# Partial sums issued between two sweeps, and another split of the FFN's blocks into groups

## The chip, the cores and the metric

The kernel runs on one core of one Trainium2 chip. The metric is the device time of one execution in microseconds (us), and the time of a kernel is the median of its runs. The engines are TensorE (PE, with its weight loads as PEld), VectorE (DVE), ScalarE (ACT), GpSimd (POOL) and SyncE (SP, which issues most of the DMA transfers).

## The reference

Two decoder layers over 512 tokens of 1024 channels. Each layer is FFN1, a token mixer and FFN2, each followed by a layer norm of a scaled residual. The change is in the FFN, which occurs four times:

```python
def swiglu(x, wg, wu, wd):
    return (jax.nn.silu(x @ wg) * (x @ wu)) @ wd

for l in range(DEPTH):
    x = layer_norm(ALPHA * x + 0.5 * swiglu(x, ffn1_wg[l], ffn1_wu[l], ffn1_wd[l]), ln_f1_g[l], ln_f1_b[l])
    mix = token_mixer(x, w_in[l], ...)
    x = layer_norm(ALPHA * x + mix, ln_mix_g[l], ln_mix_b[l])
    x = layer_norm(ALPHA * x + 0.5 * swiglu(x, ffn2_wg[l], ffn2_wu[l], ffn2_wd[l]), ln_f2_g[l], ln_f2_b[l])
```

`wg` and `wu` are 1024 x 2816, `wd` is 2816 x 1024, all float32.

## The kernel before

**Precision.** Every float32 operand is split into a high part and a low part (`act` writes the high one on ScalarE, `sub_lo`, line 225, subtracts it on VectorE), and each product is three matmuls (`mm3`, lines 228 to 230): high by high, and the two mixed ones.

**Weights.** All weights come as one stream in the order of `layer_plan`. `Stream.load` issues their DMAs on SP into `raw` (three buffers), `Stream.pump` splits them ahead of use into `hl` (four buffers), or, for the tail's chunks, into slabs `whi` and `wlo`; how far ahead is `LOOK` and its kin. `W.get` hands out a chunk and pumps, `W.done` gives it back and pumps. A slab is a 128 x 512 buffer; there are 55. A bank is one of the eight PSUM banks of 128 x 512.

**One FFN.** The 2816 hidden channels are 22 blocks of 128. `gate_up` computes one block for all 512 tokens: two banks, 24 matmuls each, and `hidden` (lines 550 to 552) applies the gate; the result `t` is 128 channels by 512 tokens. The down projection takes the blocks in two ways.

- *Groups.* 16 blocks go in two groups of eight, and within a group in pairs. A pair's down product is done with seven products of 256 tokens by 512 output channels in place of eight (`pair_operands` forms the sums and differences of the hidden blocks, `Stream.pair` those of the weights). All pairs of a group accumulate in the same banks. `pair_group` takes two sweeps over the pairs, for there are eight banks and each product needs two: first products 1, 6, 7 and 5, then 2, 4 and 3. Between them the sums of the first four are added to the residual `xt`: `u` is a copy of product 1 (line 524), and product 6, 7 and 5 are added to it or to `xt` in turn (lines 525 to 533). The weights of the second sweep are the PAIR_C chunks, split at line 311, with their difference `t4h`, `t4l` at lines 337 to 340.
- *The tail.* The last six blocks are split plainly into `hh` and `hl`, and for each of four token blocks (`tb`) and each half of the output channels (`q`) a bank collects the blocks (names `d`). `residual` (lines 419 and 420) adds it to `xt`, `ln_block` (lines 424 to 433) norms it with the vectors `gb` that `ln_load` (line 413) brings, and `fin` either transposes the token block for the next stage (`transpose_x`, lines 380 to 384) or, at the end, writes it out. `fin` of a token block is written behind the first half of the next one's matmuls; the last one is put off into the next stage's head.

**Order.** The instructions of each engine are put in an order by a list scheduler at build time: it takes them by their place in the text, and passes over one that it does not yet hold to be ready; only GpSimd's order is as written.

Of the kernel before, what the change touches and what calls it, by code (L numbers as in the profile page):

```python
# [20 lines left out]
NF = FF // 128  # L21
# [21 lines left out]
PIECE, PIECES = 256, 1  # L43
PEND_AT = 3
TAIL = 4
GROUP = 8
NGROUP = 2
LOOK_PAIR = 4

PASS, STAY, TAIL_KIND, PAIR_A, PAIR_B, PAIR_C = range(6)  # L50
# [74 lines left out]
def layer_plan(l):  # L125


    p = []

    def add(c, kind=PASS):  # L130
        p.append((c, kind))

    def down(name, nkb):
        n = nkb // 2
        for dh in range(2):
            for i in range(n):
                add(down_chunk(name, l, dh, i), TAIL_KIND if dh == 1 and i >= n - TAIL else PASS)

    def tok(c0, c1):
        for c in tok_chunks(l, c0, c1):  # L140
            add(c)

    def ffn(n):
        at = 0
        for g in range(NGROUP + 1):
            end = at + GROUP if g < NGROUP else NF
            for fi in range(at, end):
                add(stat_chunk(n + "_wg", l, fi * 128))
                add(stat_chunk(n + "_wu", l, fi * 128))
            pairs = range(at // 2, end // 2)  # L150
            at = end
            if g < NGROUP:
                for j in pairs:
                    add(pair_chunk(n + "_wd", l, j, 0), PAIR_A)
                    add(pair_chunk(n + "_wd", l, j, 1), PAIR_B)
                for j in pairs:
                    add(pair_chunk(n + "_wd", l, j, 2), PAIR_C)
            else:
                for j in pairs:
                    for dh in range(2):  # L160
                        add(down_chunk(n + "_wd", l, dh, j), TAIL_KIND)

    ffn("ffn1")
    for m in range(4):
        add(gate_chunk(l, "m", m))
    tok(COL_A, COL_B)
    tok(COL_B, COL_C)
    add(uq_chunk(l, 0))
    add(uq_chunk(l, 1))
    add(ukv_chunk(l, 0), STAY)  # L170
    add(ukv_chunk(l, 1))
    for n in SCHEDULE:
        if n == "keys":
            tok(COL_C, COL_D)
        elif n == "v0":
            tok(COL_D, COL_GM)
        elif n[0] in "mn" and n[-1] == "a":
            add(gate_chunk(l, n[0], int(n[1])))
        elif n[:2] == "cw":
            add(w1_chunk(l, int(n[2]), int(n[3])))  # L180
        elif n == "c2":
            add(w2_chunk(l))
        elif n[0] == "p" and n[1] in "0246":
            add(proj_chunk(l, "w_proj_mla", int(n[1])))
    for m in range(0, KB, 2):
        add(proj_chunk(l, "w_proj_nsa", m))
    down("w_out", KB)
    ffn("ffn2")
    return p

# [10 lines left out]
def hybrid_kernel(ctx: ExitStack, tc: tile.TileContext, x, wflat, lnp, rmsg, small, cst, out):  # L201
# [8 lines left out]
    def slab(name, dt=F32):  # L210
        return slabs.tile([128, 512], dt, tag="slab", name=name)
# [284 lines left out]
    def pair_group(ops, p0, wname, l, c):  # L496

        bs = {}

        def product(n, p, lhs, w, a, first, final):  # L500
            for s in range(2):
                cols = slice(s * 128, (s + 1) * 128)
                if (n, s) not in bs:
                    bs[n, s] = bank(f"d{n}")
                lh, ll = ops[p][lhs]
                hi, lo = w
                mm3(bs[n, s], lh[:, cols], ll[:, cols], hi[:, a:a + 512], lo[:, a:a + 512], first, final)

        u = {}
        last = len(ops) - 1  # L510
        for p in range(len(ops)):
            ta = W.get(pair_chunk(wname, l, p0 + p, 0))
            tb = W.get(pair_chunk(wname, l, p0 + p, 1))
            wa, wb = [(t[:, 0, :], t[:, 1, :]) for t in (ta, tb)]
            f, z = p == 0, p == last
            product(1, p, "a11", wa, 0, f, z)
            product(6, p, "s2", wa, 512, f, z)
            W.done()
            product(7, p, "s3", wb, 512, f, z)
            product(5, p, "s1", wb, 0, f, z)  # L520
            W.done()
        for s in range(2):
            u[s] = slab("u")
            act(out=u[s], in_=bs[1, s], func=AF.Copy)  # L524
            stt(out=xt[s, 0], in0=xt[s, 0], scalar=float(c), in1=u[s], op0=ALU.mult, op1=ALU.add)
            tt(out=u[s], in0=u[s], in1=bs[6, s], op=ALU.add)
        for s in range(2):
            stt(out=xt[s, 1], in0=xt[s, 1], scalar=float(c), in1=u[s], op0=ALU.mult, op1=ALU.add)
            tt(out=u[s], in0=u[s], in1=bs[7, s], op=ALU.add)
            stt(out=xt[2 + s, 1], in0=xt[2 + s, 1], scalar=float(c), in1=u[s], op0=ALU.mult, op1=ALU.add)  # L530
            tt(out=xt[2 + s, 1], in0=xt[2 + s, 1], in1=bs[5, s], op=ALU.add)
            tt(out=xt[s, 1], in0=xt[s, 1], in1=bs[5, s], op=ALU.add)
            stt(out=xt[2 + s, 0], in0=xt[2 + s, 0], scalar=float(c), in1=u[s], op0=ALU.mult, op1=ALU.add)
        for p in range(len(ops)):
            t, h, lo = W.get(pair_chunk(wname, l, p0 + p, 2))
            wc = t[:, 0, :], t[:, 1, :]
            f, z = p == 0, p == last
            product(2, p, "a12", wc, 0, f, z)
            product(4, p, "a22", (h, lo), 0, f, z)
            product(3, p, "s4", wc, 512, f, z)  # L540
            W.done()
        for s in range(2):
            tt(out=xt[s, 0], in0=xt[s, 0], in1=bs[2, s], op=ALU.add)
            tt(out=xt[2 + s, 0], in0=xt[2 + s, 0], in1=bs[4, s], op=ALU.subtract)
            tt(out=xt[s, 1], in0=xt[s, 1], in1=bs[3, s], op=ALU.add)

    def ffn(l, n, ln_idx, last):
        def hidden(g, u):
            t = slab("t")
            act(out=t, in_=g, func=AF.Tanh, scale=0.5)  # L550
            stt(out=t, in0=t, scalar=1.0, in1=g, op0=ALU.add, op1=ALU.mult)  # L551
            tt(out=t, in0=t, in1=u, op=ALU.mult)  # L552
            return t

        chunks = [[stat_chunk(n + w, l, fi * 128) for w in ("_wg", "_wu")] for fi in range(NF)]

        def gate_up(fi):
            gu = []
            for c in chunks[fi]:
                gu.append(bank("gu"))  # L560
                stat_mms(gu[-1], W.get(c), 0, T, range(KB), True, True)
                W.done()
            return hidden(*gu)

        heads = head_tiles(chunks[0] + chunks[1], "ffh")
        c = 4 * ALPHA
        for g in range(NGROUP):
            ops = []
            for i in range(GROUP // 2):
                fi = g * GROUP + 2 * i  # L570
                if fi == 0:
                    a, b = hidden(*heads[0:2]), hidden(*heads[2:4])
                else:
                    a = gate_up(fi)
                    b = gate_up(fi + 1)
                ops.append(pair_operands(a, b))
            pair_group(ops, g * GROUP // 2, n + "_wd", l, c)
            c = 1.0
        hT = []
        for fi in range(NGROUP * GROUP, NF):  # L580
            t = gate_up(fi)
            h, lo = slab(f"hh{fi}", F32R), slab(f"hl{fi}", F32R)
            act(out=h, in_=t, func=AF.Copy)
            sub_lo(lo, t, h)
            hT.append((h, lo))
        gb = ln_load(ln_idx, l)
        chs = [[W.get(down_chunk(n + "_wd", l, dh, i)) for dh in range(2)] for i in range(NGROUP * GROUP // 2, NF // 2)]

        def fin(tb):
            if last:  # L590
                for q in range(2):
                    nc.sync.dma_start(out=out[tb * 128:(tb + 1) * 128, q * 512:(q + 1) * 512], in_=xt[tb, q])
            else:
                transpose_x(tb)

        for tb in range(TB):
            st = work.tile([128, 2, 6], F32, tag=f"st{tb}", bufs=1, name="st")
            cols = slice(tb * 128, (tb + 1) * 128)
            for q in range(2):
                b = bank(f"d{q}{tb}")  # L600
                for k, (lh, ll) in enumerate(hT):
                    ch, j = chs[k // 2][q], (k % 2) * 512
                    mm3(b, lh[:, cols], ll[:, cols], ch.h(j, j + 512), ch.l(j, j + 512), k == 0, k == len(hT) - 1)
                if q == 0 and tb:
                    fin(tb - 1)
                residual(tb, q, b, 1.0, st)
            ln_block(tb, st, 16 * LN_EPS, gb)
        if last:
            fin(TB - 1)
        else:  # L610
            pend.append(lambda: fin(TB - 1))
# [829 lines left out]
```

## Time and profile before

| what | us |
|---|---|
| median of 3 runs | 2266.36 |
| lowest, highest run | 2266.27, 2270.03 |
| the profiled execution | 2265.32 |
| its span, first to last instruction | 2263.5 |
| mean granted clock of TensorE | 0.992 of full |

The rows below are from the profiled execution; times in them count from its span's start. Busy time of PE counts overlapping matmuls once, so the step from one start to the next says more than a duration.

### The profile page before, as it was taken

What the parts mean: (1) busy time and instruction counts of PE and PEld (TensorE: products, weight loads), DVE (VectorE), ACT (ScalarE), POOL (GpSimd) and SP (SyncE); (2) the same over time, 40 slices, a digit from 0 to 9 for tenths busy, and PEclk for the clock granted to TensorE, in tenths of its full rate; (3) what the DMA queues carried; (4) which work ended last, traced back from release to release, by engine and by line L of the source; (5) the groups of instructions that cost most, each with busy time, mean ns of one, the idle gap of its engine ahead of it and who ended that gap; (6) DMA issues with size and microseconds to landing.
All of it is one profiled execution on the core that took longest, in us unless ns stands there. A gap on an engine that the chain in (4) does not pass through costs nothing. (4 is left out here: it accounts for less than half of the span.)

```text
span 2263.5 us, 29587 instructions
## 1 busy us (share of the span) xinstructions
PE 2219.9 (98%) x11162; PEld 1896.1 (84%) x11162; DVE 1500.0 (66%) x2842; ACT 956.8 (42%) x1798; POOL 102.5 (5%) x166
## 2 busy tenths in 40 slices
PE   9999999999999999999999999999999999999998
PEld 8878788998888887878788787889988889878786
DVE  4675845577887658475656657555688966584845
ACT  3333331469774233342223333314697742333431
POOL 0000001010002000000000000010100010000000
PEclk9999999999999999999999999999999999999999
DMA  5243442444225233333423324423532262232332
GB/s 177 85 125 93 124 127 100 134 123 137 96 84 199 94 106 122 99 115 99 130 66 101 119 83 135 143 95 103 153 123 99 71 243 74 94 121 98 107 115 81
DMA packets 90943, 259.99 MB, mean 115 GB/s; under 512 B 18736, under 2 KB 21936, under 8 KB 90800
## 3 DMA queue, kind: packets, MB, share of 16 engines
q1 hardware_dynamic: 79888, 222.96, 31.2%
q0 software_dynamic: 10624, 34.61, 4.3%
q8 instruction: 88, 1.44, 0.3%
q10 hardware_dynamic: 288, 0.52, 0.1%
q14 instruction: 55, 0.45, 0.1%
HBM read 233.94 MB, written 24.12 MB: 114 GB/s over the span
## 5 line engine op out<-in xcount | busy, mean ns | idle before, releaser
L225 DVE TENSOR_TENSOR hl<-raw,hl 128x1024 fp32r<-128x1024 f32 (+4 forms) x379 | 431.2, 1144 | 211.7 <-ACT hl L302 166.7
L302 ACT ACTIVATE hl<-raw 128x1024 fp32r<-128x1024 f32 (+2 forms) x283 | 288.8, 1022 | 514.2 <-issue 250.2
L229 PE MATMUL gu<-xTl,hl 128*128 128x512 f32 x1280 | 498.7, 390 | 0.0
L228 PE MATMUL gu<-xTh,hl 128*128 128x512 f32 x1280 | 498.6, 390 | 0.0
L230 PE MATMUL gu<-xTh,hl 128*128 128x512 f32 x1280 | 498.6, 390 | 0.0
L230 PEld LDWEIGHTS gu<-xTh,hl 128*128 128x128 f32 x1280 | 240.4, 188 | 49.8
L229 PEld LDWEIGHTS gu<-xTl,hl 128*128 128x128 f32 x1280 | 240.4, 188 | 49.6
L228 PEld LDWEIGHTS gu<-xTh,hl 128*128 128x128 f32 x1280 | 240.4, 188 | 49.5
L552 DVE TENSOR_TENSOR t<-t,gu 128x512 f32<-128x512 f32 x80 | 55.0, 688 | 174.0 <-PE gu L230 174.0
L551 DVE SCALAR_TENSOR_TENSOR t<-t,gu 128x512 f32<-128x512 f32 x80 | 54.9, 686 | 156.2 <-ACT t L550 156.2
L550 ACT ACTIVATE t<-gu 128x512 f32<-128x512 f32 x80 | 47.5, 593 | 212.0 <-PE gu L230 212.0
L311 ACT ACTIVATE hl<-raw 128x512 fp32r<-128x512 f32 (+1 forms) x96 | 86.5, 916 | 111.5 <-PE gu L230 82.7
L659 ACT ACTIVATE P<-P,nm 128x384 f32<-128x384 f32 x192 | 105.6, 552 | 38.6 <-DVE nm L657 34.0
L229 PE MATMUL d<-hl,ph_s 128*128 128x512 f32 x256 | 99.7, 390 | 0.0
L228 PE MATMUL d<-hl,ph_s 128*128 128x512 f32 x256 | 99.7, 390 | 0.0
L230 PE MATMUL d<-hl,pl_s 128*128 128x512 f32 x256 | 99.7, 389 | 0.0
L383 ACT ACTIVATE xTh<-xtp 128x512 fp32r<-128x512 f32 x48 | 26.9, 597 | 169.8 <-PE xtp L380 169.2
L225 DVE TENSOR_TENSOR pl<-pt,ph 128x512 fp32r<-128x512 f32 x144 | 79.2, 595 | 25.5 <-ACT ph L683 25.0
L427 POOL TENSOR_TENSOR rs<-rs,ct 128x1 f32<-128x1 f32 x24 | 22.3, 929 | 1559.2 <-DVE rs L426 1559.2
L657 DVE CUSTOM_DVE_ANT_0 P<-sc,maskw 128x384 f32<-128x384 f32 x192 | 82.9, 485 | 2.5 <-PE sc L651 2.3
L229 PE MATMUL d<-wlo,hh 128*128 128x512 f32 x192 | 75.5, 393 | 3.1 <-DVE wlo L225 3.1
L228 PE MATMUL gf<-xTh,hl 128*128 128x512 f32 x192 | 77.3, 402 | 0.0
(366 smaller groups left out, 4676.1 us busy)
## 6 DMA issues: line engine op xcount, KB each, us to landing
raw<-in_wflat_dram SPq DMA_DIRECT2D x343, 512.0 KB, 3.6
raw<-in_wflat_dram SPq DMA_DIRECT2D x36, 256.0 KB, 2.6
gb<-in_lnp_dram SPq DMA_DIRECT2D x24, 256.0 KB, 5.4
raw<-in_wflat_dram SPq DMA_DIRECT2D x12, 384.0 KB, 3.1
sy<-gl POOLq DMA_DIRECT2D x16, 256.0 KB, 2.8
xr<-spill SPq DMA_DIRECT2D x16, 256.0 KB, 5.8
ym<-sy POOLq DMA_DIRECT2D x16, 256.0 KB, 6.1
raw<-in_wflat_dram SPq DMA_DIRECT2D x8, 416.0 KB, 3.8
```

Source lines behind the costliest of these rows:

```text
L225: tt(out=o, in0=src, in1=f(hi), op=ALU.subtract)
L228: mm(o, lh, rh, start=start, stop=False)
L229: mm(o, lh, rl, start=False, stop=False)
L230: mm(o, ll, rh, start=False, stop=stop)
L302: act(out=h, in_=r[:, j:j + e], func=AF.Copy)
L311: act(out=hi, in_=r, func=AF.Copy)
L383: act(out=h, in_=bv, func=AF.Copy)
L550: act(out=t, in_=g, func=AF.Tanh, scale=0.5)
L551: stt(out=t, in0=t, scalar=1.0, in1=g, op0=ALU.add, op1=ALU.mult)
L552: tt(out=t, in0=t, in1=u, op=ALU.mult)
L657: nc.vector.tensor_tensor_reduce(out=o, in0=ps[b][:, off:off + n], in1=maskw[:, T - n:T], scale=1.0, scalar=BIG, op0=ALU.add, op1=ALU.min, ...
L659: act(out=o, in_=o, func=AF.Exp, bias=self.nm[:, qb:qb + 1], scale=-1.0, accum_out=self.l[:, qb:qb + 1])
```

## The change

Four things. The group sizes are ten and eight, which leaves four blocks for the tail. In the last pair of a first sweep, the copies of product 1 are written directly behind product 1, and the additions of products 6 and 7 directly behind those products, ahead of `W.done`; those of product 5 stay behind the sweep. In the tail, both banks of a token block are taken at once; for token block 0 the matmuls of the last hidden block stand behind those of the other three in both halves; for the others the order is first half, `fin` of the block before, residual, second half.

```diff
-GROUP = 8
-NGROUP = 2
+GROUPS = (10, 8)
...
     def ffn(n):
         at = 0
-        for g in range(NGROUP + 1):
-            end = at + GROUP if g < NGROUP else NF
+        for g in GROUPS + (0,):
+            end = at + g if g else NF
...
-            if g < NGROUP:
+            if g:
...
             product(1, p, "a11", wa, 0, f, z)
+            if z:
+                for s in range(2):
+                    u[s] = slab("u")
+                    act(out=u[s], in_=bs[1, s], func=AF.Copy)
             product(6, p, "s2", wa, 512, f, z)
+            if z:
+                for s in range(2):
+                    stt(out=xt[s, 0], in0=xt[s, 0], scalar=float(c), in1=u[s], op0=ALU.mult, op1=ALU.add)
+                    tt(out=u[s], in0=u[s], in1=bs[6, s], op=ALU.add)
             W.done()
             product(7, p, "s3", wb, 512, f, z)
+            if z:
+                for s in range(2):
+                    stt(out=xt[s, 1], in0=xt[s, 1], scalar=float(c), in1=u[s], op0=ALU.mult, op1=ALU.add)
+                    tt(out=u[s], in0=u[s], in1=bs[7, s], op=ALU.add)
             product(5, p, "s1", wb, 0, f, z)
             W.done()
         for s in range(2):
-            u[s] = slab("u")
-            act(out=u[s], in_=bs[1, s], func=AF.Copy)
-            stt(out=xt[s, 0], in0=xt[s, 0], scalar=float(c), in1=u[s], op0=ALU.mult, op1=ALU.add)
-            tt(out=u[s], in0=u[s], in1=bs[6, s], op=ALU.add)
-        for s in range(2):
-            stt(out=xt[s, 1], in0=xt[s, 1], scalar=float(c), in1=u[s], op0=ALU.mult, op1=ALU.add)
-            tt(out=u[s], in0=u[s], in1=bs[7, s], op=ALU.add)
             stt(out=xt[2 + s, 1], in0=xt[2 + s, 1], scalar=float(c), in1=u[s], op0=ALU.mult, op1=ALU.add)
...
-        for g in range(NGROUP):
+        done = 0
+        for g in GROUPS:
             ops = []
-            for i in range(GROUP // 2):
-                fi = g * GROUP + 2 * i
+            for fi in range(done, done + g, 2):
...
-        for fi in range(NGROUP * GROUP, NF):
+        for fi in range(done, NF):
...
-            for q in range(2):
-                b = bank(f"d{q}{tb}")
-                for k, (lh, ll) in enumerate(hT):
+            bs = [bank(f"d{q}{tb}") for q in range(2)]
+
+            def part(q, ks):
+                for k in ks:
+                    lh, ll = hT[k]
                     ch, j = chs[k // 2][q], (k % 2) * 512
-                    mm3(b, lh[:, cols], ll[:, cols], ch.h(j, j + 512), ch.l(j, j + 512), k == 0, k == len(hT) - 1)
-                if q == 0 and tb:
-                    fin(tb - 1)
-                residual(tb, q, b, 1.0, st)
+                    mm3(bs[q], lh[:, cols], ll[:, cols], ch.h(j, j + 512), ch.l(j, j + 512), k == 0, k == len(hT) - 1)
+
+
+            late = len(hT) - (tb == 0)
+            part(0, range(late))
+            if tb:
+                fin(tb - 1)
+                residual(tb, 0, bs[0], 1.0, st)
+            part(1, range(late))
+            if not tb:
+                part(0, range(late, len(hT)))
+                residual(tb, 0, bs[0], 1.0, st)
+                part(1, range(late, len(hT)))
+            residual(tb, 1, bs[1], 1.0, st)
             ln_block(tb, st, 16 * LN_EPS, gb)
```

## Rows read from the trace of the kernel before

**Rows 1.** The page, span and part 1: busy time, share of the span and instructions of each engine.

```profile
span 2263.5 us, 29587 instructions
PE 2219.9 (98%) x11162; PEld 1896.1 (84%) x11162; DVE 1500.0 (66%) x2842; ACT 956.8 (42%) x1798; POOL 102.5 (5%) x166
```

**Rows 2.** What the matmul engine (PE) waited for over the whole span: who waited, for whom, us in total, times, longest us.

```profile
PE d L228 <- ACT u L524: 19.4, 8, 2.7
...
PE d L229 <- DVE wlo L225: 3.1, 6, 0.8
...
PE d L228 <- DVE u L526: 0.2, 1, 0.2
```

**Rows 3.** Instructions in order of time around the end of a first sweep (ffn2 of layer 0, first group): start us, us, engine, line, operation, out<-in, count, and in brackets the idle time before it with what ended it. PE's rows come first, then ScalarE's (ACT), then VectorE's (DVE).

```profile
885.03 0.39 PE L230 MATMUL d<-hl,pl_s 128*128 128x512 f32 x1
887.75 0.50 PE L228 MATMUL d<-hl,ph_a 128*128 128x512 f32 x1 [2.33 <-ACT u L524]
...
889.69 0.39 PE L230 MATMUL d<-hl,pl_a 128*128 128x512 f32 x1
890.28 0.50 PE L228 MATMUL d<-t4h,ph_a 128*128 128x512 f32 x1 [0.20 <-DVE u L526]
...
883.02 1.06 ACT L311 ACTIVATE hl<-raw 128x1024 fp32r<-128x1024 f32 x1 [0.66 <-DMA raw<-in_wflat_dram]
884.07 0.63 ACT L339 ACTIVATE t4h<-t 128x512 fp32r<-128x512 f32 x1
885.50 1.06 ACT L311 ACTIVATE hl<-raw 128x1024 fp32r<-128x1024 f32 x1 [0.81 <-PE d L230]
886.58 0.63 ACT L339 ACTIVATE t4h<-t 128x512 fp32r<-128x512 f32 x1
887.12 1.07 ACT L524 ACTIVATE u<-d 128x512 f32<-128x512 f32 x2
...
881.01 0.69 DVE L337 TENSOR_TENSOR t<-t,raw 128x512 f32<-128x512 f32 x1
...
888.34 1.28 DVE L525 SCALAR_TENSOR_TENSOR xr<-xr,u 128x512 f32<-128x512 f32 x2
...
897.34 0.68 DVE L532 TENSOR_TENSOR xr<-xr,d 128x512 f32<-128x512 f32 x1
897.94 2.35 DVE L225 TENSOR_TENSOR hl<-raw,hl 128x1024 fp32r<-128x1024 f32 x2
```

**Rows 4.** PE alone in eight stretches, one for each group: from the start of the last matmul of the first sweep to the start of the 36th matmul after it. Columns: stretch, its us, PE busy us (instructions that touch it), granted clock, DMA share, GB/s; the last row sums all eight.

```profile
121.84:134.60 12.76, 10.06 (x37) 0.87 0.37 113
...
885.03:896.32 11.29, 8.77 (x37) 1.00 0.38 128
...
2136.18:2148.42 12.24, 10.04 (x38) 0.86 0.34 113
sum 98.66, PE 79.06; mean PE 9.88
```

**Rows 5.** The tail of ffn2 of layer 0, token blocks 0 and 1, in order of time, columns as in rows 3: PE from the first matmul of block 1 to its 18th and the eight transposes behind it; then VectorE.

```profile
1109.24 0.39 PE L228 MATMUL d<-whi,hh 128*128 128x512 f32 x1
...
1113.10 0.39 PE L230 MATMUL d<-whi,hl 128*128 128x512 f32 x1
1113.33 1.32 PE L380 MATMUL xtp<-ident,xr 128*128 128x128 f32 x8
...
1109.44 0.69 DVE L419 SCALAR_TENSOR_TENSOR xr<-xr,d 128x512 f32<-128x512 f32 x1 [0.22 <-PE d L230]
...
1112.53 1.41 DVE L433 SCALAR_TENSOR_TENSOR xr<-xr,rs,gb 128x512 f32<-128x512 f32 x2
1113.85 0.68 DVE L419 SCALAR_TENSOR_TENSOR xr<-xr,d 128x512 f32<-128x512 f32 x1
...
1115.18 1.27 DVE L225 TENSOR_TENSOR xTl<-xtp,xTh 128x512 fp32r<-128x512 f32 x2
```

**Rows 6.** PE alone in three stretches of 36 matmuls from the wait for `wlo` in the tails of ffn1 and ffn2 of layer 0 and ffn1 of layer 1, columns as in rows 4; the last row sums all three.

```profile
1106.32:1115.41 9.09, 8.10 (x37) 1.00 0.61 203
...
sum 27.53, PE 24.38; mean PE 8.13
```

**Rows 7.** Busy time of each engine in a stretch between two sweeps and in one of hidden blocks alone: stretch, its us, then busy us (instructions) of PE, PEld, DVE, ACT and POOL, granted clock, DMA share, GB/s.

```profile
881.00:900.00 19.00, 16.48 (x72) 12.99 (x71) 18.87 (x28) 7.41 (x10) 0.00 (x0) 1.00 0.40 134
910.00:925.00 15.00, 15.00 (x68) 12.44 (x67) 5.74 (x6) 4.16 (x5) 0.00 (x0) 1.00 0.23 76
```

**Rows 8.** VectorE's operations by shape from 860 to 870 us: line, engine, operation, out<-in, shapes, count, busy us, mean ns, idle before.

```profile
L328 DVE TENSOR_TENSOR raw<-raw 128x512 f32<-128x512 f32 x2 | 1.4, 690 | 0.0
...
L225 DVE TENSOR_TENSOR hl<-raw,hl 128x1024 fp32r<-128x1024 f32 x1 | 1.2, 1226 | 0.0
...
L481 DVE TENSOR_TENSOR s<-t 128x256 f32<-128x256 f32 x1 | 0.4, 424 | 0.0
```

**Rows 9.** From the last matmul of the last hidden block to its operand in the tail of ffn2 of layer 0 (columns as in rows 3), and the landing times of the norm's vectors `gb` (issued at line 413).

```profile
1099.29 0.39 PE L230 MATMUL gu<-xTh,hl 128*128 128x512 f32 x1
...
1101.40 0.69 DVE L225 TENSOR_TENSOR hl<-t,hh 128x512 fp32r<-128x512 f32 x1 [0.70 <-ACT hh L583]
...
DMA to landing us min/median/max: 4.8/5.4/6.5
```

More of the change, by code (lines that the diff above doesn't have):

```diff
@@ L576, in ffn @@
                 ops.append(pair_operands(a, b))
-            pair_group(ops, g * GROUP // 2, n + "_wd", l, c)
+            pair_group(ops, done // 2, n + "_wd", l, c)
+            done += g
             c = 1.0
         hT = []
-        for fi in range(NGROUP * GROUP, NF):
+        for fi in range(done, NF):
             t = gate_up(fi)
@@ L586, in ffn @@
         gb = ln_load(ln_idx, l)
-        chs = [[W.get(down_chunk(n + "_wd", l, dh, i)) for dh in range(2)] for i in range(NGROUP * GROUP // 2, NF // 2)]
+        chs = [[W.get(down_chunk(n + "_wd", l, dh, i)) for dh in range(2)] for i in range(done // 2, NF // 2)]
         def fin(tb):
```

## The prediction

> **What bounds the kernel now.** I read the page first: the matmul engine (PE) is busy for 2219.9 of 2263.5 us, VectorE for two thirds, ScalarE for less than half [rows 1]. So the time is PE's work, plus what PE loses to waits and to its clock. The list of PE's waits came next: 19.4 us, over half of all its waiting, is one wait that comes eight times, the first matmul after a group's first sweep for ScalarE's copy `u` [rows 2]. There are eight groups in the kernel (four FFNs, two groups each). Then the order of time around one of them [rows 3]. The first sweep's last matmul starts at 885.03 and the next one, product 2, only at 887.75. It needs the bank that product 1 held, product 1 was over some 4 us earlier, and the copy that empties its bank runs at 887.12, behind the split of a second-sweep weight that itself waited for the sweep's last product (885.50). ScalarE was idle for 0.66 and 0.81 us shortly before. The copy is late by its place in ScalarE's order, not for want of time.
>
> Last I took PE's own stretches. One matmul of 512 columns follows the next at 0.227 us: 17 steps between 1109.24 and 1113.10 [rows 5]. The duration column says 0.39, but the matmuls overlap, so every price below goes by 0.227. The eight stretches of 36 matmuls behind the stalls take 98.66 us together [rows 4]; 288 x 0.227 = 65.4, so 33.3 us are lost, well over the 19.4 that the waits show. The rest is the clock: where it stayed at 1.00 (885.03) the loss is 11.29 - 8.17 = 3.1 us; in the others, granted 0.86 to 0.87 on average, it is 4.0 to 4.6 us, for PE ran at the lower of its two levels (1.2 instead of 2.4 GHz) for a while after it had stood still.
>
> **The change, part by part.** *Fewer matmuls.* A pair of blocks costs 7 products x 2 x 3 = 42 matmuls; two blocks in the tail cost 2 x 4 x 2 x 3 = 48. One more pair for each FFN saves 6, four FFNs 24: 24 x 0.227 = **5.4 us**. Nothing else on PE changes in number.
>
> *The sums, moved and not added.* The two copies now stand behind product 1 of the last pair, the sums of products 6 and 7 behind those products, and the weight splits that the two `done` calls release come after them. Product 1 ends 18 matmuls (4.1 us) before the sweep does, the two copies take 1.07 us [rows 3], and so the bank is free some 3 us before product 2 wants it. Product 4 wants product 6's bank 6 matmuls later: four VectorE operations at 0.60 us (16 sums take 888.34 to 897.94) after an event 2.7 us before the sweep's end. This too fits, if barely, because VectorE is full there: 18.87 of 19 us [rows 7]. What is late next, then, is VectorE's other work, the splits of the second sweep. From 881.01 it does three of them by 888.34 (7.3 us), the 16 sums (9.6 us), and the first two gate splits [rows 3]. Eight sums ahead of the third and fourth split push the fourth to 888.34 + 4.8 = 893.1; the second sweep, now starting at 885.26, wants it after three pairs of 18 matmuls, at 897.5. The first gate split still lands at 897.94 + 1.2 = 899.2, against 885.26 + 72 x 0.227 = 901.6. Four and two microseconds of slack; if either were gone, PE would wait by the overrun. With five pairs the second sweep is 4.1 us longer and the sums are not, so the group of ten has more room. I therefore take the stalls as removed, clock included, **33.3 us**, and charge what is left between nothing and the one wait for `u` of VectorE, whose matmul started 0.59 after the one before, 0.36 more than the pitch [rows 3]: 0.3 each, **+2.4 us** (0 to 2.9).
>
> *The extra pair's VectorE work.* Splits and differences of a pair's weights are eight operations of 0.69 to 1.23 us and five small ones of 0.42 plus three of 0.69 for its operands, some 12 us; two tail blocks cost six of 0.69, 4 us [rows 8]. The 8 us per FFN lie beside the hidden blocks' matmuls, where VectorE is busy for 5.74 of 15 us [rows 7]; without that cover it would be 32 us. Per FFN the weights are one load and 256 KB more on SP's queue, with the DMA engines at 0.23 there: nothing. The slabs: five pairs hold 35, the residual 8, weight differences and temporaries under 8, of 55; nothing, but see the last rival.
>
> *The tail.* Its four weight chunks, no longer six, all lie within the look-ahead of five, so the late sixth goes. The three stretches from the wait for `wlo` take 27.53 us for 108 matmuls [rows 6], 24.5 at the pitch: **3.0 us** saved. The last hidden block's operand starts its last step 2.1 us after the block's last matmul starts and takes 0.69 [rows 9]; three blocks and both halves of token block 0 are 18 matmuls, 4.1 us, so `late` covers it, as 15 did before; without it 9 matmuls (2.0 us) would not. `gb` is needed some 6.7 us after it is issued (24 matmuls and 1.3 of residual) and lands in 6.5 at most [rows 9]: nothing.
>
> *The tail's transposes* are where the change can cost. Now a block's 18 matmuls run, then the transposes of the block before. These need the norm, which VectorE begins at 1109.44 and whose first half ends at about 1113.2; PE gets there at 1113.33 [rows 5]: covered to 0.1 us. With four blocks only 12 matmuls, 2.7 us, stand in front. In written order PE waits 1.2 us at each of three blocks of three FFNs (the last FFN transposes nothing): 9 x 1.2 = 10.8 us. But the order on PE isn't the written one: at 889.69 a third matmul trio of `ph_a`, of the next pair, runs ahead of the `t4h` product that is written before it and isn't ready [rows 3]. Part 1's 12 matmuls are ready and can go ahead likewise. Per token block VectorE needs 4.4 us (1109.44 to 1113.85), 1.3 for the first half's residual and 1.27 for the transposed low parts, 7.0 in all, against 24 x 0.227 + 1.1 = 6.5 us of PE; a lag of 1.5 us over three blocks is taken up by the next stage's matmuls. Between 0 and 1.2 I take 0.4, nearer the row that shows reordering with a remainder of 0.36: **+3.6 us** (0 to 10.8). At the kernel's end the same lag shows: **+0.4 us**.
>
> The Trainium skill ("TensorE: Matmul & The Clock Gate", "Step-by-step: what each phase is for") says that matmuls stay in program order and only weight loads are pulled ahead. By that rule alone a transpose issued too early holds back all behind it, and the sum would have 10.8 in place of 3.6. It speaks of the issued order; rows 3 show that the issued order isn't the written one.
>
> **The sum** is made against the profiled execution, 2265.3 us with a span of 2263.5; the runs' median is 1.0 us above it. 2265.3 - 33.3 - 5.4 - 3.0 = 2223.6, and + 2.4 + 3.6 + 0.4 = **2230.0 us**.
>
> **Rivals.** *The transposes wait:* the written order holds in the tail: 2223.6 + 2.4 + 10.8 + 0.4 = 2237, and 1.2 more at each of the nine if the clock falls there too: 2248. Against the clock: the `wlo` waits left it at 1.00 [rows 6].
>
> *A shorter stall stays:* VectorE does the third and fourth split before product 6's sums, as now. Then product 6's bank comes free at about 890.2 [rows 3] where PE, with six matmuls of the next pair pulled ahead, wants it at 888.0: 2.2 us, and 1.3 for the clock, eight times 28: 2223.6 + 28 + 4 = 2256. For it: VectorE is full. Against it: the sums are now written first, and need only products that are over.
>
> *It doesn't do what it says:* the copies still come behind the last split in ScalarE's order. Only 5.4 + 3.0 are gained: 2257, and about 2261 with the tail's waits.
>
> *Slower:* the group of ten runs out of slabs. The place is the first sweep: with all 55 held, each next pair's weight difference waits until the pair before frees its three, and then about 4.5 us of VectorE and ScalarE steps lie bare, at four pairs of four FFNs 72 us: 2223.6 + 72 + 4 = 2300. It decides from 55 live slabs on; I count about 50.
>
> **How the numbers follow.** Forecast 0.68 (its own range 2222 to 2238), transposes wait 0.12, shorter stall 0.10, doesn't do it 0.06, slabs 0.04. The forecast alone gives 2230. Most of the transposes' case lies under 2248; the shorter stall and what is beyond, 0.20, are left out: **2221 to 2248**. A measurement of this kernel tells about 0.2%, 4.5 us, from no change. All but the slab case are faster by more than that, except a part of "doesn't do it" around 2261: faster 0.94, same 0.02, slower 0.04.
>
> **What would show it.** Right: no wait of PE for `u` of ScalarE, the granted clock at 1.00 around the eight transitions, no `wlo` wait, 24 fewer matmuls. The tail shows transposes after more than 12 matmuls, or waits for the norm (`xr`, line 433). Wrong would be: PE waiting for `hl` or `t4h` in the second sweep (splits late behind sums), or for `t2` in the first sweep of ten (slabs).

## The result

The changed kernel takes 2239.4 us (median of 4 runs, 2238.2 to 2239.9) against 2267.7 of the kernel before in the same rounds: a ratio of 0.9873, with a 95% interval of 0.9856 to 0.9891. A second comparison on one chip gave 0.9879 (0.9864 to 0.9895). The profiled execution took 2239.7 us. So it is faster by some 28 us; 35 were forecast.

The page of the changed kernel, span and part 1, answering [rows 1]:

```profile
span 2237.9 us, 29650 instructions
PE 2204.3 (99%) x11138; PEld 1883.8 (84%) x11138; DVE 1525.0 (68%) x2886; ACT 966.9 (43%) x1810; POOL 102.8 (5%) x166
```

24 matmuls fewer, as counted. What PE waited for, answering [rows 2] (who, for whom: us in total, times, longest):

```profile
PE xtp L379 <- DVE xr L432: 8.3, 6, 1.7
PE xtp L379 <- DVE x L432: 4.2, 3, 1.7
...
PE d L227 <- DVE u L530: 1.0, 3, 0.4
```

The eight waits for ScalarE's `u` and the six for `wlo` are gone. In their place stand nine waits of the transposes (`xtp`) for the norm's last step, `xr` or `x` of line 432 (433 before), 12.5 us in all, which the kernel before did not have once.

The transitions themselves are what was wanted. PE over the same eight stretches of 36 matmuls behind each first sweep, answering [rows 4], columns as there:

```profile
148.15:156.67 8.52, 8.44 (x37) 1.00 0.30 95
...
1034.16:1043.01 8.85, 8.45 (x37) 1.00 0.33 113
...
sum 68.88, PE 67.58; mean PE 8.45
```

98.66 us became 68.88, and the granted clock is 1.00 in all eight. One of them in order of time (second group of ffn2, layer 0), answering [rows 3], ScalarE, VectorE and then PE:

```profile
1031.72 1.07 ACT L519 ACTIVATE u<-d 128x512 f32<-128x512 f32 x2
1032.68 1.06 ACT L310 ACTIVATE hl<-raw 128x1024 fp32r<-128x1024 f32 x1
...
1032.80 1.29 DVE L523 SCALAR_TENSOR_TENSOR xr<-xr,u 128x512 f32<-128x512 f32 x2
1034.01 1.28 DVE L524 TENSOR_TENSOR u<-u,d 128x512 f32<-128x512 f32 x2
1035.20 1.22 DVE L224 TENSOR_TENSOR hl<-raw,hl 128x1024 fp32r<-128x1024 f32 x1
...
1034.16 0.39 PE L229 MATMUL d<-hl,pl_s 128*128 128x512 f32 x1
1034.39 0.39 PE L227 MATMUL d<-hl,ph_a 128*128 128x512 f32 x1
...
1038.70 0.39 PE L228 MATMUL d<-t4l,ph_a 128*128 128x512 f32 x1
1039.48 0.50 PE L227 MATMUL d<-hl,ph_s 128*128 128x512 f32 x1 [0.40 <-DVE u L530]
```

The copies run at 1031.72, ahead of the split that they used to follow, and the second sweep starts one step (0.23 us) behind the first. What remains is product 3 at 1039.48, which waits 0.40 us for the sums of product 7: VectorE had put weight work between them, the split at 1035.20 first.

The loss is in the tail (ffn2 of layer 0, PE and then VectorE), answering [rows 5]:

```profile
1100.36 0.39 PE L227 MATMUL d<-whi,hh 128*128 128x512 f32 x1
...
1102.85 0.39 PE L229 MATMUL d<-whi,hl 128*128 128x512 f32 x1
1104.91 1.32 PE L379 MATMUL xtp<-ident,xr 128*128 128x128 f32 x8 [1.68 <-DVE xr L432]
...
1099.88 1.37 DVE L418 SCALAR_TENSOR_TENSOR xr<-xr,d 128x512 f32<-128x512 f32 x2 [1.79 <-PE d L229]
1101.16 1.28 DVE L419 BATCH_NORM_STATS2 st<-xr 128x6 f32<-128x512 f32 x2
...
1104.11 1.41 DVE L432 SCALAR_TENSOR_TENSOR xr<-xr,rs,gb 128x512 f32<-128x512 f32 x2
```

Twelve matmuls of token block 1 (1100.36 to 1102.85), then the transposes of block 0, which need the norm's first half. That ends at 1104.8. PE stands still until then, though the twelve matmuls of the second half are ready. The transposes of the other two blocks wait 1.20 and 1.30 us in the same way.

### The profile page after: what moved, and what is told of

The parts are those of the page before. It is cut to its first block, busy times and chain, and to the rows that moved or that the text cites. A ratio compares the mean times of both kernels' runs of the same rounds, so it can differ in the third digit from the quotient of the medians.

```text
span 2237.9 us, 29650 instructions
## 1 busy us (share of the span) xinstructions
PE 2204.3 (99%) x11138; PEld 1883.8 (84%) x11138; DVE 1525.0 (68%) x2886; ACT 966.9 (43%) x1810; POOL 102.8 (5%) x166
## 5 line engine op out<-in xcount | busy, mean ns | idle before, releaser
L224 DVE TENSOR_TENSOR hl<-raw,hl 128x1024 fp32r<-128x1024 f32 (+5 forms) x391 | 443.4, 1140 | 211.2 <-ACT hl L301 165.6
L310 ACT ACTIVATE hl<-raw 128x1024 fp32r<-128x1024 f32 (+1 forms) x108 | 97.5, 916 | 123.8 <-PE gu L229 85.4
L227 PE MATMUL d<-hl,ph_s 128*128 128x512 f32 x288 | 113.0, 392 | 1.3 <-DVE u L530 1.0
L228 PE MATMUL d<-hl,ph_s 128*128 128x512 f32 x288 | 112.1, 389 | 0.0
L229 PE MATMUL d<-hl,pl_s 128*128 128x512 f32 x288 | 112.1, 389 | 0.0
L227 PE MATMUL gf<-xTh,hl 128*128 128x512 f32 x192 | 77.2, 402 | 0.0
L229 PE MATMUL gf<-xTh,hl 128*128 128x512 f32 x192 | 75.2, 392 | 0.0
```

The source lines that it names most:

```text
L224: tt(out=o, in0=src, in1=f(hi), op=ALU.subtract)
L227: mm(o, lh, rh, start=start, stop=False)
L228: mm(o, lh, rl, start=False, stop=False)
L229: mm(o, ll, rh, start=False, stop=stop)
L310: act(out=hi, in_=r, func=AF.Copy)
```

## The experiments

All were timed against the kernel before on the same chip; ratios are to that. Waits are those of PE.

**The transposes behind both halves.** In the changed kernel; the residual of the new block's first half thereby stands ahead of the transposes too:

```diff
             part(0, range(late))
             if tb:
-                fin(tb - 1)
                 residual(tb, 0, bs[0], 1.0, st)
             part(1, range(late))
+            if tb:
+                fin(tb - 1)
```

> The changed kernel with the transposes of the block before written behind both halves (24 matmuls) in place of the first half (12). Theory A (the place is the cause: the norm takes about 4.5 us from the last matmul, 12 matmuls cover 2.7): the nine waits for xr, 14.0 us with what is lost around them, and the half-rate stretch at about 350 us, 1.3, go; some 2224 us against the changed kernel's 2239.4. Rival B (VectorE's work per token block, 7.0 us, is more than PE's 6.5, so the loss only moves): waits of about the same size show elsewhere in the tail or in the next stage's head, 2235 us or more.

Measured: 2223.3 us, 0.9817 (0.9802 to 0.9832), with no stretch at the lower level in the FFNs.

```profile
PE xtp L379 <- DVE xr L432: 1.8, 2, 0.9
...
PE xtp L379 <- DVE x L432: 0.9, 1, 0.9
```

Six of the nine waits are gone, as theory A has it, and the time is where it put it. Three of 0.9 us are left, one in each tail, at the third transposes. So B has a share: VectorE's lag is there, but it is worth 2.7 us and not 14.

**The transposes behind 18 matmuls.** To see whether the wait follows the place step by step:

```diff
-                fin(tb - 1)
                 residual(tb, 0, bs[0], 1.0, st)
-            part(1, range(late))
+                part(1, range(2))
+                fin(tb - 1)
+                part(1, range(2, late))
             if not tb:
+                part(1, range(late))
```

> The changed kernel with the transposes written behind 18 matmuls (the first half and two of the second half's four blocks) in place of 12. Theory A (the order on PE keeps to the written place here, and the wait is the norm's length less what stands in front): each wait shrinks by 6 x 0.227 = 1.36 us: 1.84, 1.36 and 1.46 lost per tail become about 0.5, nothing and some tenths (VectorE's lag adds to the last), some 3 us in all against 14; about 2226 us where the changed kernel takes 2239. Rival B (the order on PE is not tied to the written place): the same waits as with 12 or none.

Measured: 2223.6 us, 0.9814 (0.9798 to 0.9829), against 0.9879 of the changed kernel on the same chip. The waits that are left:

```profile
PE xtp L379 <- DVE xr L432: 0.4, 2, 0.2
PE xtp L379 <- DVE x L432: 0.2, 1, 0.2
```

PE in the tail of ffn2 of layer 0, from the first matmul of token block 1:

```profile
1096.75 0.39 PE L227 MATMUL d<-whi,hh 128*128 128x512 f32 x1
...
1101.05 0.39 PE L228 MATMUL d<-wlo,hh 128*128 128x512 f32 x1
1101.30 0.66 PE L379 MATMUL xtp<-ident,xr 128*128 128x128 f32 x4
1101.71 0.48 PE L229 MATMUL d<-whi,hl 128*128 128x512 f32 x1
1102.03 0.60 PE L379 MATMUL xtp<-ident,xr 128*128 128x128 f32 x4
...
1103.16 0.40 PE L227 MATMUL d<-whi,hh 128*128 128x512 f32 x1
...
1108.39 0.39 PE L229 MATMUL d<-whi,hl 128*128 128x512 f32 x1
1108.88 1.32 PE L379 MATMUL xtp<-ident,xr 128*128 128x128 f32 x8
...
1115.87 1.23 PE L379 MATMUL xtp<-ident,xr 128*128 128x128 f32 x8 [0.20 <-DVE xr L432]
```

With 12, 18 and 24 matmuls written in front of the transposes, the waits are 12.5, 0.6 and 2.7 us. But here PE did not run the transposes at the written place. The first four stand behind 20 matmuls of their block (1096.75 to 1101.05) and the other four behind one more, and those of the next two blocks behind all 24 (1103.16 to 1108.39); the other two tails have the same order. So the condition of theory A falls and that of rival B holds: the order on PE is not tied to the written place here. This kernel comes near the one with the transposes behind both halves, and its time can't be told from that one's (0.9814 and 0.9817). A kernel with a tail of four blocks in which the transposes run behind 18 was thus not measured.

**The sums alone.** The kernel before with nothing but the sums moved (the first block of the diff in `pair_group`; groups of eight, a tail of six in the old order).

> The kernel before with the sums moved and nothing else: groups of eight, tail of six, old order in the tail. Theory A (the sums alone end the eight stalls, 33.3 us with the clock, less 1.5 that stay as waits for u of VectorE; 18 matmuls still cover the norm in the tail): about 2235 us, below the whole change, no wait for xr at the transposes, the wlo waits still there. Rival B (the stalls went because the groups changed): 2260 us or more with waits for u of ScalarE.

Measured: 2237.9 us, 0.9880 (0.9864 to 0.9896), where about 2235 was expected.

```profile
PE d L229 <- DVE wlo L225: 3.0, 5, 0.8
PE d L228 <- ACT whi L302: 1.5, 2, 1.1
PE d L228 <- DVE u L531: 1.3, 3, 0.8
```

No wait for `u` of ScalarE, none at the transposes. The moved sums carry the whole gain: the changed kernel (0.9873 and 0.9879) can't be told from this one. The 18 matmuls of a six-block half still cover the norm.

**The groups and the tail alone.** The changed kernel with the sums back behind the first sweep.

> The changed kernel with the sums back behind the whole sweep: groups of ten and eight and the new tail stay. Theory A: eight waits for u of ScalarE of about 2.4 us come back with seven or eight half-rate stretches, 31 to 33 us more than the changed kernel, about 2271 us; that is no faster than the kernel before, for the tail's waits (15) eat the 8.4 us that fewer matmuls and the absent wlo waits give. Rival B (the larger group alone helps the stalls): under 2260 us.

Measured: 2267.2 us, 1.0015 (1.0005 to 1.0025).

```profile
PE d L227 <- ACT u L523: 19.7, 8, 2.6
PE xtp L379 <- DVE xr L432: 8.4, 6, 1.7
PE xtp L379 <- DVE x L432: 4.2, 3, 1.7
```

The stalls are back, with the lower clock behind five of the eight, and the rest of the change by itself gives nothing: what fewer matmuls and the absent `wlo` waits save, the transposes' waits take.

**Without the late block.** The changed kernel with `late = len(hT)` for all token blocks.

> The changed kernel without the late last block for the first tokens. Theory A (9 matmuls cover 2.0 us and the last block's operand needs 2.8): a wait of under 1 us for hl at the start of each of four tails, but the first half's residual then runs beside the second half's matmuls, and the first of the three transpose waits falls from 1.8 to about 1.3 us in three tails: within 3 us of the changed kernel. Rival B (late is what makes the transposes wait): the waits for xr go and it takes 2228 us or less.

Measured: 2235.1 us, 0.9871 (0.9856 to 0.9887). The start of the tail of ffn2 of layer 0 on PE (block 0's first half begins at 1092.71), and its first transposes:

```profile
1094.98 0.39 PE L228 MATMUL d<-wlo,hh 128*128 128x512 f32 x1
1095.20 0.39 PE L227 MATMUL d<-whi,hh 128*128 128x512 f32 x1
1095.43 0.39 PE L228 MATMUL d<-wlo,hh 128*128 128x512 f32 x1
1095.66 0.78 PE L229 MATMUL d<-whi,hl 128*128 128x512 f32 x2
...
1102.46 1.32 PE L379 MATMUL xtp<-ident,xr 128*128 128x128 f32 x8 [1.21 <-DVE xr L432]
```

There is no wait at the tail's start, against theory A. The one matmul that needs the last block's low part `hl` has been passed over: the first two matmuls of the second half run at 1095.20 and 1095.43, and the third product of either half's trio follows at 1095.66, with under 0.2 us lost. The order on PE had found its own cover, in the same tail in which it left the transposes where they were written. The other part of theory A holds: the first transposes wait 1.21 and not 1.68 us, since with late the two residuals stand back to back behind block 0's end (lines 418 and 419, from 1099.88 to 1102.4 in the changed kernel). In the time this does not show: 0.9871 against 0.9873 and 0.9879.

**Both.** The transposes behind both halves and no late block.

> Transposes behind both halves and no late last block. Theory A (late only puts the two residuals of token block 0 back to back behind its end, which starts VectorE's lag in the tail 0.5 us deeper; the order on PE covers the last block's operand without it): the third transpose wait of each of three tails, 1.1 us, shrinks to about 0.6, no wait for hl at the tail's start: 1 to 2 us less than with late, about 0.9810 of the kernel before. Rival (late pays): a wait for hl of about 0.8 us in four tails, 2 to 3 us more than with late, 0.9830.

Measured: 2220.9 us, 0.9799 (0.9786 to 0.9812), with the next one the fastest. No wait for `xr` or `hl` is left in the tails. The only waits in the four FFNs behind their heads:

```profile
PE d L227 <- DVE u L530: 0.6, 2, 0.4
```

**Two blocks' transposes put off.** As above, with those of token block 2 in the next stage's head as well (`fin` for `tb < TB - 1` only, and a second `pend.append`).

> As the one before, and the transposes of token block 2 are put off into the next stage's head too, as those of block 3 are. Theory A (what is left in the tail is VectorE's lag of 7.0 against 6.5 us per block, which shows at the last transposes alone): no wait for xr at all, 2 us less, 0.9805. Rival (the lag only moves into the head): PE waits for xr or hl in the head, same time as the one before.

Measured: 2220.95 us, 0.9800 (0.9786 to 0.9813): no difference, since the lag was already hidden without the late block. It tells nothing on the rival.

**Groups of twelve and six.** The first experiment's kernel with `GROUPS = (12, 6)`.

> Transposes behind both halves, groups of twelve and six in place of ten and eight; as many matmuls. Theory A (slabs: about 50 of 55 are live at ten, so 57 would be needed at twelve): PE waits around the last hidden blocks of the first group or in its first sweep, several us in each of four FFNs, and more half-rate stretches: 2240 us or more. Rival (slabs are no limit there): within 3 us of the version with ten and eight, but in the group of six, where 16 sums and three splits lie beside a second sweep of 54 matmuls (12.2 us), waits for hl of about 2 us in each of four FFNs.

Measured: 2224.3 us, 0.9814 (0.9801 to 0.9827), with the same waits at the same places as with ten and eight (2.7 us for `xr` and `x`). Theory A falls: even six pairs don't make PE wait for slabs, so at five the limit was not near. The rival's waits in the group of six did not come either.

**Eight more VectorE operations at each transition.** In the first experiment's kernel, behind the sums of product 7; their result goes nowhere:

```diff
                     tt(out=u[s], in0=u[s], in1=bs[7, s], op=ALU.add)
+                more = slab("more")
+                for _ in range(8):
+                    tt(out=more, in0=u[0], in1=u[1], op=ALU.add)
```

> Transposes behind both halves, and eight more VectorE additions (0.60 us each, 4.8 us, their result unused) behind the sums of product 7 at each of the eight transitions. The prediction put VectorE's slack before the first gate split at 2 us with groups of eight and about 6 with ten. Theory A (so it is): waits for hl of 2 to 3 us at the end of the second sweep in the four groups of eight, none in the groups of ten, with the clock 10 to 18 us more than without. Rival (VectorE has more slack than that): under 4 us more. Rival on the other side (none at all): waits at all eight, 40 us or more.

Measured: 2230.1 us, 0.9840 (0.9826 to 0.9853), some 5 us more than without.

```profile
PE gu L229 <- DVE hl L224: 2.7, 4, 0.7
```

The four waits end behind the second sweeps of the four groups of eight (at 297.7, 1047.2, 1401.8 and 2153.3 us); the groups of ten have none. So the place was right and the size was not: the waits are 0.7 us each where theory A had 2 to 3, and the clock stays up behind all four. The slack is thus about 4.8 - 0.7 = 4.1 us, an estimate, about twice what the prediction had. The waits explain 3 of the 5 us; a stretch at the lower clock level (half rate) in the second mixer, which these kernels have in some executions and not in others, is in the rest.

## Why the prediction was right, and where it was off

| term | forecast, us | measured, us |
|---|---|---|
| eight stalls with their clock, less what stays | -33.3 + 2.4 | 68.88 - 98.66 = -29.8 |
| 24 matmuls | -5.4 | 24 fewer, -5.4 |
| waits for `wlo` | -3.0 | gone, -4.9 |
| the tail's transposes | +3.6 | +13.9, and +1.6 for the clock |
| last matmul to the end | +0.4 | 9.0 to 9.5, +0.5 |
| sum | -35.3 | -24.1; the span fell by 25.6 |

The 13.9 are the steps from the twelfth matmul to the transposes less the pitch: 1.84, 1.36 and 1.45 us in each of three tails. The 1.6 are eight steps of 0.427 in place of 0.227 us behind one of the waits: that tail takes 31.56 us on PE, the other two 29.96 each. Of the 1.5 us that the last line leaves, 1.0 is an earlier start (the first gate matmul at 8.4 and not 9.4 us, after a shorter wait for `x`) and 0.2 the two mixers together.

**The stalls.** Right in mechanism and, to 1.1 us, in size. The two kernels with one part each settle it: with the sums alone the stalls go, with all but the sums they stay.

**VectorE beside the second sweep.** It held with more room than worked out (4.1 us for 2). Part of the difference shows in the run with eight more operations: the gate's first four matmuls (1045.46 to 1046.14) run ahead of the one that needs the split's low part and waits until 1047.20, so the split was needed 0.9 us later than the prediction took it.

**The waits for `wlo`.** They went as forecast, but were priced too low. Each stretch of [rows 6] was counted as 36 matmuls of 512 columns, and eight of its instructions are transposes (those at 1113.33 in [rows 5]), which take 1.1 us and not 8 x 0.227. Counted by the steps around the waits in the kernel before:

```profile
1106.32 0.40 PE L228 MATMUL d<-whi,hh 128*128 128x512 f32 x1
1107.47 0.50 PE L229 MATMUL d<-wlo,hh 128*128 128x512 f32 x1 [0.76 <-DVE wlo L225]
...
1108.67 0.50 PE L229 MATMUL d<-wlo,hh 128*128 128x512 f32 x1 [0.23 <-DVE wlo L225]
```

From 1106.32 to 1109.24 [rows 5] are six steps in 2.92 us, 1.56 more than the pitch gives; with 1.69 and 1.70 in the other two tails that is 4.9 us. That this and the earlier start brought the measured time some 3 us nearer to the forecast is luck.

**The transposes.** Here a step failed. The prediction had the price for the written order, 10.8 us, as its upper end, and chose 0.4 for each wait, because one row of the second sweep showed matmuls run ahead of a product that wasn't ready. From "the order on PE isn't the written one" it did not follow that it would be bent *here*. In the changed kernel it wasn't: in all three tails the transposes stand behind the 12 matmuls where they were written, and the term came to 13.9 us of waits and 1.6 of clock in place of 3.6. Why is not shown. It is not that the scheduler never passes over transposes, for written behind 18 matmuls they ran behind 20 to 24; but there the residual of the new block's first half was written ahead of them as well, and the two moves were not tried apart. What the runs do show is that the transposes need the norm, that 12 matmuls don't cover it, and that written behind more of them they wait 2.7 us or less in all. The rival "the transposes wait" is what happened, at 2239.7 where it gave 2237. Its 10.8 us were 4.7 too few: 1.6 are the half-rate stretch, 1.4 the late block, which puts two residuals behind block 0's end (the first wait is 1.84 with it, 1.36 without), and the rest that no wait cost less than 1.36 where it had 1.2; the `wlo` waits and the earlier start hid part of it.

**The late block.** That 9 matmuls would not cover the last block's operand was wrong, because there the order did adapt. So late, taken as a cover without cost, covered under 0.2 us here. What it costs shows in the waits, not clearly in the time: the first transposes wait 1.68 us with it and 1.21 without, and with the transposes behind both halves the three waits of 0.9 us are there with it and not without; the times there are 2223.3 and 2220.9 us, in ratios whose intervals overlap (0.9817 and 0.9799).

**The slabs.** The count of 50 was not refuted at ten, but twelve, which would have made it 57, ran as well. So the count was too high, or slabs come free earlier than it assumed; which of the two no run here tells.

**The clock.** That the half-rate stretches go with the stalls was right. That a wait of some 1.2 us leaves the clock alone was right for the six transpose waits of 1.2 to 1.3 us; the other three were 1.68 us long, and the clock fell after one of them.

## What to carry to other kernels

When a tail is made shorter, the dependent work that its matmuls covered doesn't get shorter with it: count the matmuls in front of each consumer again (here 18 covered the norm to 0.1 us, 12 did not) and write the consumer behind more of them. A place where a list scheduler adapted says nothing of the next place, nor of the same instructions written a little later (held at 12 matmuls here, moved on from 18); price the written order, move the text, and read the order that came of it in the trace: two moved lines and a dropped special case took 0.9873 to 0.9799. And what empties a bank for the next phase belongs directly behind the product that fills it, ahead of any prefetch that the same engine could do later.

## What the runs showed of the hardware

Standing still does not always bring the clock down, and the length of the wait alone doesn't tell when. In the changed kernel the first transposes of three tails wait 1.68 us each, behind the same 36 matmuls. After one of them PE ran at the lower level, after the other two it did not; PE in the stretches behind them (columns as above):

```profile
350.00:353.50 3.50, 3.50 (x10) 0.54 0.00 0
1106.50:1110.00 3.50, 3.50 (x17) 1.00 0.00 0
1464.50:1468.00 3.50, 3.50 (x17) 1.00 0.00 0
```

Ten matmuls against seventeen in the same 3.5 us. In a second execution of the same kernel the clock fell after none of the three. A stall's clock is thus a price with a chance. Of the eight stalls for `u` in the kernel before, 2.20 to 2.70 us long, the clock fell after seven [rows 4]: after the two of 2.20, and not after the one of 2.33 (887.75). Where the sums were put back it fell after five of 2.32 to 2.61 us, and not after three of 2.36, 2.63 and 2.63. In the kernel with the sums alone it fell once in a tail, after waits of 1.06 and 0.84 us that end 1.3 us apart (1448.31 and 1449.65).
